# The opening of a two-layer mLSTM and attention backbone: modulation loads, the last 512 tokens' load, and the order of the first projections

## The chip, the cores and the metric

The kernel runs on one core of one Trainium2 chip. The metric is the device time of one execution in microseconds (us). The time before is the median of three runs: 2864.13 us (2863.14 to 2865.72).

The core has a matrix engine (TensorE, PE in the profile; its weight loads are PEld), a vector engine (DVE), a scalar engine (ACT), GpSimd (POOL) and SyncE (SP), which here issues the DMA transfers. Each engine works through its own instructions in order and waits on semaphores for the others.

## The reference

1024 latent tokens and 256 context tokens of width 1024 go through two layers. Each layer normalizes, modulates with vectors that a product of the conditioning with `w_ada` gives, projects with one input matrix, mixes (mLSTM heads and neighbourhood attention), projects out, and runs a squared-ReLU MLP. What the change touches is the start of layer 0:

```python
mod = silu_c @ w_ada[l] + b_ada[l]
mod_c = silu_cc @ w_ada[l] + b_ada[l]
sh1, sc1, g1, sh2, sc2, g2 = jnp.split(mod[:, None, :], N_MOD, axis=-1)
...
h = rmsnorm(x, norm1_g[l]) * (1.0 + sc1) + sh1
hc = rmsnorm(xc, norm1_g[l]) * (1.0 + sc1c) + sh1c
y, yc = token_mixers(h @ w_in[l], hc @ w_in[l], ...)
```

So before the first projection of a token there are its sum of squares, its reciprocal root, and the shift and gain of each feature, which need a pass over 8 MB of `w_ada`.

## The kernel before

**Data.** Activations lie with features on the partitions: eight feature tiles of 128, and three groups of tokens along the free axis: the 256 context tokens (group 0), latent tokens 0 to 511 (group 1) and 512 to 1023 (group 2). In the program's names, x_146 and x_147 are group 0's features 0 to 3 and 4 to 7, x_148 and x_149 those of group 1, x_150 and x_151 those of group 2. `A = range(4)` and `B = range(4, 8)` in `opening` are the lower and the upper four features.

**Products in three parts.** Every float32 factor is split into a rounded high half and a low half: `split_raw` does it for weights (`whi` on ACT, L88; `wlo` on DVE, L89), `parts` for activations (`ah` on ACT, L1112; `al` on DVE, L1113). One product is then three matrix products (L94, L95, L96), of which the last needs the low half of the activation.

**The modulation.** `ada(0, (0, 2), "mm", ap0, 6)` and `ada(0, (1, 3), ...)` are two generators, `first` and `second`: shift and gain of features 0 to 3, and of 4 to 7. Each goes through eight loads of 512 KB (`wada`, L174) in six buffers that both share. `steps(g, n)` advances one: a step multiplies a load that came six steps earlier on PE (`through`, L158, four products, eight rows in the profile) and issues the next load, as long as there is one. The fifteenth step copies the sums (L185), transposes them on PE (L188) and adds the bias and the gain (L192, L238).

**The order of the opening** is written by hand, under `manual_schedule`, and each engine follows the order of the code: the squares of groups 0 and 1 with the product that sums them (`squares`, L1657 to L1659) and their root (`rstd`, L297 and L298); the loads of group 2 and of the third chunk of the weights for keys, values and gates (`w_kvg`); the scaling by the root (`scale`, L1664); the first modulation; then `norm` (modulation L1674 or L1676, and the two halves) and `project(i, features, u)`, which adds features into the sums of token pair i (256 tokens; pair 0 is the context, 1 and 2 are group 1, 3 and 4 group 2). The lower features of pairs 0, 1 and 2 come before the second modulation is ready, and between them stand the squares of group 2 and steps of `second`. Then come the upper features of pairs 0 to 2, the scaling of group 2, and pair 3 feature by feature.

**Behind the opening** `mixers` copies the gates (L485), turns and rotates the keys (L513, L468 to L472, with the tables cos and sin; PE transposes, L525 and L336) and projects pair 4 (L94 to L96 again). From here a scheduler orders the work. In `mixers` two DMAs store the conditioning (`sscr<-silu`, L1590), in pieces of one element; a later stage reads it. Also there, `na_values` needs the two chunks of the attention's value weights (`w_nv`), the first of which the opening already loads and splits.

Of the kernel before, what the change touches and what calls it, by code (L numbers as in the profile page):

```python
# [11 lines left out]
F32 = mybir.dt.float32  # L12
# [35 lines left out]
class Kern:  # L48
# [1537 lines left out]
    def mixers(self, l, xsrc, hi, lo, need_ctx, W, accs, Wv):  # L1586
        self.wide = 0
        if l == 0:
            for v in range(2):
                self.nc.sync.dma_start(self.sscr[v, :].rearrange("(k p) -> p k", p=128), self.silu[:, :, v])  # L1590
            self.fill = self.ada(l, range(6, 10), "q")
            self.rows = self.ada_rows(l, range(4, 6), range(2))
        self.gt, self.mst, self.nst = None, {}, {}
        with self.open(name=f"mix{l}", side="right") as self.mx:
            with self.open(name=f"mkv{l}") as self.mp:
                self.cosT = self.load(self.mx, "cos", [128, 8, 32])
                self.sinT = self.load(self.mx, "sin", [128, 8, 32])
                self.sel = self.load(self.mx, "sel", [128, 16])
                kv = self.mlstm_kv(l, hi, lo, W, accs)
                with self.open(name=f"gt{l}", side="right") as tp_:  # L1600
                    gates = self.gates(l, tp_)
                    next(gates)

                    with self.tc.issue_after(self.normed.ins) if l == 0 else contextlib.nullcontext():
                        for i in range(NT // 2):
                            next(kv)
                            if i > 2:
                                next(gates)
                        next(kv)
                    values = self.na_values(l, hi, lo, Wv + self.value_weights(l, range(len(Wv), 2)))  # L1610
                    next(gates)
                    next(gates)
                    run_all(values)
                    with self.behind():
                        run_all(gates)
                W = self.joint_weights(l, 0)
                with self.behind():
                    first = self.project_j(W, 0, hi, lo, 512 if need_ctx else 256)
                with self.open(name=f"mout{l}") as self.mb:
                    self.setup_out(l)  # L1620
                    with self.behind():
                        run_all(kv)
                    Wq, keys = self.mlstm_out(l, hi, lo, need_ctx, W, first)
            with self.open(name=f"na{l}") as self.np_:
                yh, yl = self.alloc_act()
                W, xt = [], []
                self.na(l, hi, lo, need_ctx, Wq, keys, self.ahead(l, 0 if need_ctx else 1, xsrc, yh, yl, W, xt))
        return yh, yl, W, xt

    def opening(self, xp, ap0, xsrc, hi, lo):  # L1630
# [53 lines left out]
        q, A, B, accs = [[], [], []], range(4), range(4, 8), {}  # L1684

        def project(i, ks, u):
            accs[i] = self.project_g(W, i, hi, lo, "q", accs.get(i), ks, (u,))

        run_all(squares(0, q[0]))
        more = squares(1, q[1])  # L1690
# [3 lines left out]
        steps(first, 1)  # L1694
        steps(more, 1)
        steps(first, 1)
        self.load_x(x, xsrc, (2,))
        nc.sync.dma_start(raws[2][:], d["w_kvg"][0][:, 1728:])
        r1 = self.rstd(*q[1])
        scale(0, r0)  # L1700
        for z in range(2):
# [4 lines left out]
        for z in range(6):  # L1706
            steps(first, 1)
            steps(second, 1)
        self.less_last(raws[2], chunks[2][1], 288)
        steps(first, 1)  # L1710
        norm([(0, f) for f in A])
        for u in range(2):
            project(0, A, u)
        rest = squares(2, q[2])
        norm([(1, f) for f in A])
        for i in (1, 2):
            for u in range(2):
                steps(rest, 1)
                project(i, A, u)
                steps(second, 1)  # L1720
        r2 = self.rstd(*q[2])
        W.append(self.split_raw(raws[2], chunks[2][1]))
        steps(second, 4)
        scale(2, r2, range(3))
        steps(second, 1)
        norm([(0, f) for f in B])
        for u in range(2):
            project(0, B, u)
        norm([(1, f) for f in B])
        for i in (1, 2):  # L1730
            for u in range(2):
                project(i, B, u)
        scale(2, r2, range(3, KT))
        norm([(2, f) for f in range(KT)])
        accs[3] = [self.bank("mm") for _ in range(2)]
        for k in range(KT):
            for u in range(2):
                project(3, (k,), u)
        return W, accs, self.value_weights(0, range(1))

    def run(self):
        nc, d = self.nc, self.d
        PS = bass.MemoryType.PSUM
        with self.open(name="pad", side="right") as pad, self.open(name="const") as self.cp, self.open(name="w") as self.wp, \
# [12 lines left out]
            xsrc = d["xT"]  # L1757
            hi, lo = self.alloc_act()
            with self.open(name="x0") as xp, self.open(name="sp0") as self.sp, self.open(name="ada0") as ap0, self.tc.manual_schedule():
                W, accs, Wv = self.opening(xp, ap0, xsrc, hi, lo)  # L1760
            self.ntmp = 3
            for l in range(DEPTH):
                need_ctx = l < DEPTH - 1
                groups = (0, 1, 2) if need_ctx else (1, 2)
                yh, yl, W, xt = self.mixers(l, xsrc, hi, lo, need_ctx, W, accs, Wv if l == 0 else [])
                mod, A = self.mod, self.A
                hid, xmid = hids[l], xmids[l]
                ada = chain(*(self.ada_rows(*a) for a in ((l, range(10, 12), range(2)), (l + 1, range(4), range(2)), (l + 1, range(4, 12), range(1))) if need_ctx))
# [271 lines left out]
```

## Time and profile before

| what | value |
|---|---|
| median of three runs | 2864.13 us |
| the profiled execution | 2859.85 us |
| its span, first to last instruction | 2857.9 us |
| granted PE clock, mean | 0.995 |
| instructions | 45593 |
| moved by DMA | 497.39 MB, mean 174 GB/s |

The profiled execution is one run, 4.3 us below the median of the others. Rows of the timeline give the start in us from the span's start, the duration, the engine, the source line, the operation with its output and inputs, how many such instructions the row merges, and in brackets how long the engine had been idle and what ended that. SPq is SyncE's queue of DMA issues; its durations are those of issuing. Rows of stages give the busy time of PE, PEld, DVE, ACT and POOL, then the granted clock, the DMA engines' busy share and GB/s.

### The profile page before, as it was taken

Reading aid. Unit: us, or ns where it says so; the run is one execution under the profiler, and the core shown is the slowest. Engines: PE = TensorE matmul, PEld = TensorE weight load, DVE = VectorE, ACT = ScalarE, POOL = GpSimd, SP = SyncE. Lnnn points to the kernel's source line nnn. Section 1 sums busy time; section 2 is a strip of 40 time slices with the busy share of each in tenths; the row PEclk is TensorE's granted clock in tenths of the full one; section 3 lists DMA queues with packets and bytes.
Section 4 is the critical chain, followed back from the end, with each engine's and each line's share of the span. In section 5 each row is a group of like instructions: output and inputs, shape, how many; then the busy total and the mean of one; then the engine's idle time right before and its main releaser. Section 6 shows DMA issues by size and latency. Waiting matters only on the chain. (4 is left out here: it accounts for less than half of the span.)

```text
span 2857.9 us, 45593 instructions
## 1 busy us (share of the span) xinstructions
PE 2807.8 (98%) x16560; PEld 2375.8 (83%) x16560; DVE 2201.7 (77%) x4909; ACT 1276.6 (45%) x2472; POOL 111.9 (4%) x191
## 2 busy tenths in 40 slices
PE   7999999999999999999999999999999999999998
PEld 4877778888888888888889988878988788888888
DVE  5779988776698777689878778878786887768774
ACT  4333335565453333434545333335564533344453
POOL 0100000011000000000000101000010000000000
PEclk8999999999999999999999999999999999999999
DMA  7333333336447555798977222223355454479672
GB/s 243 125 132 128 133 104 108 91 114 203 138 149 246 198 195 192 247 341 295 328 264 279 71 70 88 72 76 120 113 156 193 130 183 155 145 263 320 200 256 97
DMA packets 279263, 497.39 MB, mean 174 GB/s; under 512 B 23648, under 2 KB 119904, under 8 KB 279040
## 3 DMA queue, kind: packets, MB, share of 16 engines
q1 hardware_dynamic: 279040, 494.50, 51.8%
q8 instruction: 130, 2.13, 0.3%
q14 instruction: 93, 0.76, 0.1%
HBM read 398.82 MB, written 95.59 MB: 173 GB/s over the span
## 5 line engine op out<-in xcount | busy, mean ns | idle before, releaser
L94 PE MATMUL q<-ah,whi 128*128 128x512 f32 (+1 forms) x1472 | 549.4, 373 | 0.5 <-ACT whi L1112 0.5
L96 PE MATMUL q<-ah,wlo 128*128 128x512 f32 (+1 forms) x1472 | 547.0, 372 | 0.7 <-DVE wlo L1113 0.5
L95 PE MATMUL q<-al,whi 128*128 128x512 f32 (+1 forms) x1472 | 547.6, 372 | 0.0
L94 PE MATMUL mm<-ah,whi 128*128 128x512 f32 (+1 forms) x1120 | 387.0, 346 | 0.4 <-DVE nq L859 0.2
L95 PE MATMUL mm<-al,whi 128*128 128x512 f32 (+1 forms) x1120 | 384.8, 344 | 0.0
L96 PE MATMUL mm<-ah,wlo 128*128 128x512 f32 (+1 forms) x1120 | 384.6, 343 | 0.0
L96 PEld LDWEIGHTS q<-ah,wlo 128*128 128x128 f32 x1472 | 277.3, 188 | 49.9 <-DVE wlo L1113 1.3
L94 PEld LDWEIGHTS q<-ah,whi 128*128 128x128 f32 x1472 | 277.5, 188 | 49.7 <-issue 1.7
L95 PEld LDWEIGHTS q<-al,whi 128*128 128x128 f32 x1472 | 277.5, 189 | 48.4 <-issue 1.4
L94 PE MATMUL mm<-whi,ah 128*128 128x512 f32 (+2 forms) x832 | 308.0, 370 | 1.6 <-ACT va L810 1.6
L95 PE MATMUL mm<-wlo,ah 128*128 128x512 f32 (+2 forms) x832 | 297.9, 358 | 0.4 <-DVE wlo L89 0.3
L96 PE MATMUL mm<-whi,al 128*128 128x512 f32 (+2 forms) x832 | 297.9, 358 | 0.0
L94 PEld LDWEIGHTS mm<-ah,whi 128*128 128x128 f32 x1120 | 212.0, 189 | 28.0 <-issue 2.0
L96 PEld LDWEIGHTS mm<-ah,wlo 128*128 128x128 f32 x1120 | 212.0, 189 | 25.1 <-issue 0.2
L95 PEld LDWEIGHTS mm<-al,whi 128*128 128x128 f32 x1120 | 212.0, 189 | 24.6 <-issue 0.2
L1112 ACT CAST ah<-raw 128x512 fp32r<-128x512 f32 (+1 forms) x264 | 143.5, 566 | 126.0 <-PE q L96 51.8
L1113 DVE TENSOR_TENSOR al<-raw,ah 128x512 fp32r<-128x512 f32 (+1 forms) x264 | 157.8, 622 | 29.9 <-ACT ah L1112 29.2
L94 PEld LDWEIGHTS mm<-whi,ah 128*128 128x128 f32 x832 | 157.1, 189 | 27.1 <-ACT va L810 2.4
L96 PEld LDWEIGHTS mm<-whi,al 128*128 128x128 f32 x832 | 156.9, 189 | 23.8
L95 PEld LDWEIGHTS mm<-wlo,ah 128*128 128x128 f32 x832 | 157.3, 189 | 21.3 <-DVE wlo L89 1.8
L94 PE MATMUL q<-th,whi 128*128 128x512 f32 x384 | 150.4, 392 | 2.1 <-DVE s L1277 2.0
L95 PE MATMUL q<-x,whi 128*128 128x512 f32 x384 | 150.6, 392 | 1.1 <-DVE x L1113 1.1
(306 smaller groups left out, 5237.3 us busy)
## 6 DMA issues: line engine op xcount, KB each, us to landing
raw<-w SPq DMA_DIRECT2D x168, 512.0 KB
raw<-hid SPq DMA_DIRECT2D x104, 512.0 KB
wada<-w_adaT SPq DMA_DIRECT2D x96, 512.0 KB
wraw<-w SPq DMA_DIRECT2D x80, 512.0 KB
hid<-hb SPq DMA_DIRECT2D x128, 256.0 KB
hid<-ht SPq DMA_DIRECT2D x96, 256.0 KB
w<-gscr SPq DMA_DIRECT2D x36, 512.0 KB
wada<-w_ada SPq DMA_DIRECT2D x32, 512.0 KB
```

Source lines behind the costliest of these rows:

```text
L94: mm(out, lh, rh, start=start, stop=False, skip_group_check=True)
L95: mm(out, lh, rl, start=False, stop=False, skip_group_check=True)
L96: mm(out, ll, rh, start=False, stop=stop, skip_group_check=True)
L1112: ins = self.nc.scalar.copy(hi, src)
L1113: self.nc.vector.tensor_sub(lo, src, fview(hi))
```

## The change

It reorders the opening and two places of `mixers`; no computation is added or taken out.

- The loads of group 2 move from before the modulation loop to behind the last load of `second`. The third `w_kvg` chunk's load moves into that loop, at its fourth round.
- Two steps of `second` stand right behind the first modulation, two behind the lower features of pair 0, and one behind each of pair 1's features, which are projected one by one for both halves of the pair. The final step stands between the two halves of pair 2.
- The squares of group 2 and their root stand behind the upper features of pair 0, among the modulation of group 1's upper features. Pairs 1 and 2 then take these feature by feature.
- Sums of pair 3 come from the other bank tag by `project` itself.
- The first chunk of the value weights is only loaded in the opening; it is split in `mixers`, after the second round of keys (i == 1).
- The conditioning store is issued behind the opening's last `parts` (`issue_after` places instructions behind a given one in the order, where they are on its engine).

```diff
     def mixers(...):
         if l == 0:
-            for v in range(2):
-                self.nc.sync.dma_start(self.sscr[v, :].rearrange("(k p) -> p k", p=128), self.silu[:, :, v])
+            with self.tc.issue_after(self.normed.ins):
+                for v in range(2):
+                    self.nc.sync.dma_start(self.sscr[v, :].rearrange("(k p) -> p k", p=128), self.silu[:, :, v])
...
                             if i > 2:
                                 next(gates)
+                            if Wv and i == 1:
+                                Wv = [self.split_raw(Wv[0], 1024)]
...
     def opening(...):
-            accs[i] = self.project_g(W, i, hi, lo, "q", accs.get(i), ks, (u,))
+            accs[i] = self.project_g(W, i, hi, lo, "q" if i < 3 else "mm", accs.get(i), ks, (u,))
...
-        self.load_x(x, xsrc, (2,))
-        nc.sync.dma_start(raws[2][:], d["w_kvg"][0][:, 1728:])
         r1 = self.rstd(*q[1])
...
         for z in range(6):
             steps(first, 1)
             steps(second, 1)
-        self.less_last(raws[2], chunks[2][1], 288)
+            if z == 3:
+                nc.sync.dma_start(raws[2][:], d["w_kvg"][0][:, 1728:])
         steps(first, 1)
+        steps(second, 2)
+        self.load_x(x, xsrc, (2,))
         norm([(0, f) for f in A])
         for u in range(2):
             project(0, A, u)
-        rest = squares(2, q[2])
+        steps(second, 2)
         norm([(1, f) for f in A])
-        for i in (1, 2):
+        for f in A:
             for u in range(2):
-                steps(rest, 1)
-                project(i, A, u)
-                steps(second, 1)
-        r2 = self.rstd(*q[2])
+                project(1, (f,), u)
+            steps(second, 1)
+        self.less_last(raws[2], chunks[2][1], 288)
         W.append(self.split_raw(raws[2], chunks[2][1]))
-        steps(second, 4)
-        scale(2, r2, range(3))
+        project(2, A, 0)
         steps(second, 1)
+        project(2, A, 1)
         norm([(0, f) for f in B])
         for u in range(2):
             project(0, B, u)
-        norm([(1, f) for f in B])
-        for i in (1, 2):
-            for u in range(2):
-                project(i, B, u)
+        run_all(squares(2, q[2]))
+        norm([(1, 4), (1, 5)])
+        r2 = self.rstd(*q[2])
+        scale(2, r2, range(3))
+        norm([(1, 6), (1, 7)])
+        for f in B:
+            for i in (1, 2):
+                for u in range(2):
+                    project(i, (f,), u)
         scale(2, r2, range(3, KT))
         norm([(2, f) for f in range(KT)])
-        accs[3] = [self.bank("mm") for _ in range(2)]
-        for k in range(KT):
+        for f in range(KT):
             for u in range(2):
-                project(3, (k,), u)
-        return W, accs, self.value_weights(0, range(1))
+                project(3, (f,), u)
+        raw = self.wp.tile([128, 1024], F32, name="wraw", bufs=WRAW)
+        nc.sync.dma_start(raw[:], d["w_nv"][0, :, :1024])
+        return W, accs, raw
```

On SP, the DMA queue of the opening, from the first modulation loads on, before (x_150 and x_151 are the last 512 tokens, wada 128x2x512 the opening's modulation loads, sscr the conditioning store):

```order
L174 DMA wada<-w_ada 128x2x512 x8
L1584 DMA x_150<-xT 128x4x512
L1584 DMA x_151<-xT 128x4x512
L1698 DMA wraw_174<-w_kvg 128x576
L174 DMA wada<-w_ada 128x2x512 x6
L1590 DMA sscr<-silu 128x8x1 x2
L174 DMA wada<-w_ada 128x4x256
L174 DMA wada<-w_ada 128x2x512 x2
L74 DMA wraw<-w_nv 128x1024 x2
L174 DMA wada<-w_ada 128x4x256
L132 DMA cos<-cos 128x256
```

and in the changed kernel, at the same place:

```order
L174 DMA wada<-w_ada 128x2x512 x12
L1711 DMA wraw_174<-w_kvg 128x576
L174 DMA wada<-w_ada 128x2x512 x4
L1584 DMA x_150<-xT 128x4x512
L1584 DMA x_151<-xT 128x4x512
L1747 DMA wraw<-w_nv 128x1024
L1591 DMA sscr<-silu 128x8x1 x2
L132 DMA cos<-cos 128x256
L132 DMA sin<-sin 128x256
L132 DMA sel<-sel 128x16
L174 DMA wada<-w_ada 128x4x256
L74 DMA wraw<-w_nv 128x1024
```

All sixteen modulation loads now precede the last 512 tokens; the two stores follow these and the first value weights, and precede the rotation tables and the second value weights.

On ACT, the middle of the opening before, from the last cast of group 1's lower features (ah_97) to the modulation of the context's upper features (x_147):

```order
L1112 CAST ah_97<-x_148 128x512
L1657 ACTIVATE tmp<-x_150 128x512 x4
L1657 ACTIVATE tmp<-x_151 128x512 x4
L297 ACTIVATE ssq<-mm,eps 128x512
L298 ACTIVATE ssq<-ssq 128x512
L88 CAST whi<-wraw_174 128x576
L1676 ACTIVATE x_147<-x_147,mod,A_333 128x256
```

and in the changed kernel, from the last cast of those upper features (ah_108) to the modulation of group 1's feature 6 (the second x_149):

```order
L1112 CAST ah_108<-x_147 128x256
L1660 ACTIVATE tmp<-x_150 128x512 x4
L1660 ACTIVATE tmp<-x_151 128x512 x4
L1679 ACTIVATE x_149<-x_149,mod,A_330 128x512
L1112 CAST ah_100<-x_149 128x512
L1112 CAST ah_103<-x_149 128x512
L297 ACTIVATE ssq<-mm,eps 128x512
L298 ACTIVATE ssq<-ssq 128x512
L1679 ACTIVATE x_149<-x_149,mod,A_330 128x512
```

The eight squares of group 2 and their root moved from ahead of the second modulation's use to behind it.

On DVE, the end of the opening before, from the last low half (al_134) to the keys of the first latent pair (kt of L471 and L472):

```order
L1113 TENSOR_TENSOR al_134<-x_151,ah_110 128x512
L536 MEMSET cst 128x64
L537 MEMSET cst 128x64
L89 TENSOR_TENSOR wlo<-wraw,whi 128x1024
L513 COPY kt<-q 128x128 x2
L468 TENSOR_TENSOR ropea<-q,cos 128x128 x2
L468 TENSOR_TENSOR ropeb<-q,sin 128x128 x2
L468 TENSOR_TENSOR ropea<-q,cos 128x128
L471 TENSOR_TENSOR kt<-ropea,ropeb 128x4x32
L472 TENSOR_TENSOR kt<-ropea,ropeb 128x4x32
```

and in the changed kernel:

```order
L1113 TENSOR_TENSOR al_134<-x_151,ah_110 128x512
L513 COPY kt<-q 128x128 x2
L468 TENSOR_TENSOR ropea<-q,cos 128x128 x2
L468 TENSOR_TENSOR ropeb<-q,sin 128x128 x2
L89 TENSOR_TENSOR wlo<-wraw,whi 128x1024
L471 TENSOR_TENSOR kt<-ropea,ropeb 128x4x32
L472 TENSOR_TENSOR kt<-ropea,ropeb 128x4x32
```

The low half of the value weights stands behind the rotation's products instead of ahead of them, and the two memsets went further back.

More of the change, by code (lines that the diff above doesn't have):

```diff
@@ L1759, in run @@
             with self.open(name="x0") as xp, self.open(name="sp0") as self.sp, self.open(name="ada0") as ap0, self.tc.manual_schedule():
-                W, accs, Wv = self.opening(xp, ap0, xsrc, hi, lo)
+                W, accs, raw = self.opening(xp, ap0, xsrc, hi, lo)
             self.ntmp = 3
@@ L1764, in run @@
                 groups = (0, 1, 2) if need_ctx else (1, 2)
-                yh, yl, W, xt = self.mixers(l, xsrc, hi, lo, need_ctx, W, accs, Wv if l == 0 else [])
+                yh, yl, W, xt = self.mixers(l, xsrc, hi, lo, need_ctx, W, accs, [raw] if l == 0 else [])
                 mod, A = self.mod, self.A
```

## The prediction

> **What bounds the kernel now.** First the page's busy shares, then the waits of TensorE (PE) after the opening, which is the first 80 us. The columns of the second view are engine, tile and line, what it waited for, then us in total, times and the longest.
>
> ```profile
> PE 2807.8 (98%) x16560; PEld 2375.8 (83%) x16560; DVE 2201.7 (77%) x4909; ACT 1276.6 (45%) x2472; POOL 111.9 (4%) x191
> ```
>
> ```profile
> PE q L1028 <- DVE S L1017: 5.3, 9, 1.4
> PE q L163 <- DMA wada<-w_ada: 2.1, 2, 1.2
> ```
>
> PE is busy 98% of the span, and these are its two costliest waits in 2777 us. Behind the opening, PE sets the pace and its order is unchanged, so whatever the opening ends earlier should arrive at the end nearly whole. The question is the moment at which PE begins the first piece that the change leaves alone, the key and value projection of the last 256 tokens. That is the last row of PE's timeline (columns: start, us, instruction, idle time before it):
>
> ```profile
> 23.70 1.08 PE L158 MATMUL mm<-wada,silu 128*32 128x256 f32 x8 [0.66 <-DMA wada<-w_ada]
> 25.06 1.08 PE L158 MATMUL mm<-wada,silu 128*32 128x256 f32 x8 [0.28 <-DMA wada<-w_ada]
> 26.83 0.66 PE L188 MATMUL mm<-consts,arow 128*128 128x128 f32 x2 [0.69 <-DVE arow L185]
> 29.16 0.61 PE L94 MATMUL q<-whi,ah 128*128 128x288 f32 x1 [1.67 <-ACT ah L1112]
> ...
> 34.09 0.29 PE L96 MATMUL q<-whi,al 128*128 128x288 f32 x1
> 37.48 2.05 PE L1659 MATMUL mm<-tmp,ones 128*128 128x512 f32 x2 [3.10 <-DVE tmp L1658]
> ...
> 40.05 0.44 PE L94 MATMUL q<-whi,ah 128*128 128x288 f32 x1
> 40.29 0.44 PE L95 MATMUL q<-wlo,ah 128*128 128x288 f32 x1
> ...
> 45.64 0.29 PE L95 MATMUL q<-wlo,ah 128*128 128x288 f32 x1
> 45.77 0.29 PE L96 MATMUL q<-whi,al 128*128 128x288 f32 x1
> 46.00 0.64 PE L158 MATMUL mm<-wada,silu 128*32 128x256 f32 x8
> 46.57 1.12 PE L1659 MATMUL mm<-tmp,ones 128*128 128x512 f32 x2
> ...
> 52.41 2.37 PE L158 MATMUL mm<-wada,silu 128*32 128x256 f32 x40
> 55.92 0.41 PE L188 MATMUL mm<-consts,arow 128*128 128x128 f32 x2 [1.14 <-DVE arow L185]
> 58.00 0.40 PE L94 MATMUL q<-whi,ah 128*128 128x288 f32 x1 [1.67 <-ACT ah L1112]
> ...
> 79.81 0.38 PE L94 MATMUL q<-whi,ah 128*128 128x288 f32 x1
> ```
>
> L158 multiplies a load of the modulation weights, eight rows to a load. The second half's last loads are multiplied at 52.41, and the projection of features 4 to 7 can only start at 58.00. Products follow each other by 0.24 us around 40 us (40.05, 40.29) and by 0.13 around 45.7. Why the loads are so late stands in SP's queue and in the DMA rates over 0 to 80 us (slices of 2 us):
>
> ```profile
> 19.13 1.01 SPq L1584 DMA_DIRECT2D x<-xT  x2
> ...
> 30.48 6.91 SPq L1590 DMA_DIRECT2D sscr<-silu  x2
> ```
>
> ```profile
> GB/s 19 233 385 383 387 401 402 387 387 388 386 387 389 384 385 391 393 379 386 116 2 17 40 72 215 395 410 390 176 6 0 0 0 0 0 0 162 100 0 250
> ```
>
> The last 512 tokens (2 MB) go ahead of the second half's weights, the two conditioning stores go ahead of its last two loads, and for about 10 us (38 to 48) almost no bytes move, though there is more to load.
>
> **The change part by part.** *Loads.* Loads land 1.36 us apart (23.70 to 25.06), the first half's last at 25.06. With the tokens out of the way and a store behind, the second half's eight follow directly: 25.06 + 8 x 1.36, plus 0.77 for the third weight chunk (288 of 512 KB), gives 36.7 for the last. The tokens' halves, 2.72 us each, land at 39.4 and 42.1. Six buffers are shared, and the seventh load is released by PE's multiply of the first, at about 28.4; five loads (6 us) are then still in flight, so the queue does not run dry. I price that at nothing, between 0 and 3 us (the spare time until PE wants the last load, below).
>
> *PE up to the second modulation.* Two loads are multiplied right after the transposes (27.49). A load takes 2.37 / 5 = 0.47 us at full clock, so 0.95 at half clock; the pair ends at 29.4, nearly inside the idle time up to 29.16. The first projection's 24 products took 29.16 to 34.22 (34.09 + 0.13) and now end at 34.4. PE's 3.1 us of idle before 37.48 goes, because the squares it waited for now stand later. An L158 group between projections costs 46.57 - 45.77 - 0.13 = 0.67, with a second load behind it 1.14: 35.6. Then four times six products and one load, 4 x (6 x 0.13 + 0.67) = 5.8: 41.4. Those 24 took 0.21 us each, since most ran at half clock; if PE, now without a pause ahead of them, runs them at full clock, their second half takes 1.57 instead of some 2.6, and it is 40.3. I take 41.0; either way the last load (36.7) is there.
>
> *To the projection of features 4 to 7.* Twelve products (1.57) cover the copy of the sums, then from the transpose to the first product it is 58.00 - 55.92 = 2.08, covered by twelve more. 41.0 + 1.57 + 2.08 = 44.65 instead of 58.00: **13.35 us earlier**.
>
> *What is late next.* The squares of the last 512 tokens were ready long before; now they come behind this point, on ACT, and everything that follows is a chain of ACT and DVE:
>
> ```profile
> 35.47 4.26 ACT L1657 ACTIVATE tmp<-x 128x512 f32<-128x512 f32 x8
> 50.93 0.69 ACT L297 ACTIVATE ssq<-mm,eps 128x512 f32<-128x512 f32 x1 [11.20 <-PE mm L1659]
> 51.65 0.63 ACT L298 ACTIVATE ssq<-ssq 128x512 f32<-128x512 f32 x1
> ...
> 59.56 0.41 ACT L1112 CAST ah<-x 128x256 fp32r<-128x256 f32 x1 [0.51 <-DVE x L1674]
> 59.88 0.81 ACT L1676 ACTIVATE x<-x,mod,A 128x512 f32<-128x512 f32 x1
> 60.72 0.62 ACT L1112 CAST ah<-x 128x512 fp32r<-128x512 f32 x1
> ```
>
> ```profile
> 39.76 0.69 DVE L1658 TENSOR_TENSOR tmp<-tmp 128x512 f32<-128x512 f32 x1 [0.35 <-ACT tmp L1657]
> ...
> 63.21 0.54 DVE L1674 TENSOR_SCALAR x<-x,A,mod 128x512 f32<-128x512 f32 x1
> 63.67 1.46 DVE L1113 TENSOR_TENSOR al<-x,ah 128x512 fp32r<-128x512 f32 x2
> 65.05 3.09 DVE L1664 TENSOR_TENSOR x<-x,ssq 128x512 f32<-128x512 f32 x5
> 68.06 0.54 DVE L1674 TENSOR_SCALAR x<-x,A,mod 128x512 f32<-128x512 f32 x1
> ...
> 74.03 1.47 DVE L1113 TENSOR_TENSOR al<-x,ah 128x512 fp32r<-128x512 f32 x2
> 75.76 1.51 DVE L89 TENSOR_TENSOR wlo<-wraw,whi 128x1024 fp32r<-128x1024 f32 x1
> ...
> 78.39 0.28 DVE L468 TENSOR_TENSOR ropea<-q,cos 128x128 f32<-128x128 f32 x1
> 78.58 0.28 DVE L471 TENSOR_TENSOR kt<-ropea,ropeb 128x128 f32<-128x128 f32 x1
> 78.78 0.28 DVE L472 TENSOR_TENSOR kt<-ropea,ropeb 128x128 f32<-128x128 f32 x1
> ```
>
> The context's casts end at 59.97 - 13.35 = 46.6; the eight squares take 4.26 (50.9; the tokens landed at 42.1), the last addition 0.7 (51.6), its product 1.12 (52.75). Meanwhile ACT does one modulation (0.81) and two casts (0.62 and about 0.55) until 52.9. Logarithm and exponential: 52.28 - 50.93 = 1.35, so 54.25. On DVE three scales at 0.60 (1.81), a modulation (63.67 - 63.21 = 0.46) and two subtractions (65.05 - 63.67 = 1.38) give 57.9, where the five remaining scales start. Before they started at 65.05. From there the order is the old one: 75.50 - 65.05 = 10.45 us, all DVE, to the last low half: **68.35 instead of 75.50**. So of 13.35 us, 6.2 are given back, because the squares (4.3) with their sum and root (3.3), formerly beside PE's second half, now stand in the chain. PE, which sees its products feature by feature, is ready earlier than DVE from here on.
>
> *The value split later.* From the last low half to the second rotated key was 79.06 - 75.50 = 3.56 us. The split (L89) stays inside that stretch, now behind the rotation's products; only two memsets (75.76 - 75.50 = 0.26) and one extra rope product (78.58 - 78.39 = 0.19) leave: 3.11. Its price is bounded by 0 and 1.5 (its duration, if ACT's half came late); I take 0, since ACT has only four small copies ahead of its half, and DVE six products. What queues behind the later split are the next weight loads, released at 71 instead of 77, still ahead of the old times.
>
> *The sum*: 7.15 + 0.45 = 7.6; I use **7.5 us**. The profiled execution took 2859.85 us (span 2857.9), so it would be 2852.35. The median of the runs is 2864.13, 4.3 above that execution; the same 7.5 off it gives **2856.6**, which I predict.
>
> **The clock as a term.** The columns that matter here are the granted clock and, behind it, DMA share and GB/s:
>
> ```profile
> 40.00:42.00 2.00, 2.00 (x11) 2.00 (x9) 0.46 (x1) 0.00 (x0) 0.00 (x0) 0.50 0.26 2
> ...
> 58.00:60.00 2.00, 2.00 (x9) 1.29 (x9) 1.49 (x4) 1.49 (x5) 0.00 (x0) 1.00 0.02 6
> 60.00:62.00 2.00, 2.00 (x9) 1.86 (x10) 1.57 (x3) 1.97 (x4) 0.19 (x3) 0.59 0.00 0
> 62.00:64.00 2.00, 2.00 (x11) 2.00 (x10) 1.47 (x4) 1.30 (x4) 0.00 (x0) 0.56 0.00 0
> ```
>
> After idle pieces of 1.14 and 1.67 us (rows 55.92 and 58.00), PE ran at half clock from 60.4 to 63.6. The changed order leaves PE pauses of up to 1.8 us near 49 to 52 and near 61, and 3 us before the keys, so such stretches can come there. The Trainium skill, "TensorE: Matmul & The Clock Gate", section "Why this matters for your kernels", asks only for no idle gap above about 3 us between bursts. By that the pauses inside the opening would never halve the clock. The trace here disagrees with it, since 1.67 us sufficed; by the rule the sum stays as it is, by the trace the first rival below has a chance.
>
> **The rivals.**
> - *Half clock takes part back* (15%). A stretch of 3.2 us at 0.24 instead of 0.13 us a product costs 13 products against 25: 1.5 us each. Around 50 us it is hidden by the DVE chain; one in the last DVE-bound stretch and one in the next projection cost 3 together: 2859.6. For it speaks 60 to 64 above; against it that the 3 us pause before 79.81 did not do it before.
> - *The change does not bring the second half forward enough* (8%). If the shared buffers let the queue run dry, each us beyond 41 at which the last load lands is a us lost; 4 us late gives 2860.6. Against it: from 10 to 18 us, before the tokens were issued, such loads ran at 385 to 400 GB/s.
> - *It is hidden anyway* (8%): the next stage has a wait that does not move, such as weights that now load in another order: 2863 to 2864. Against it: the few waits quoted above.
> - *Slower* (7%): the stores, now issued behind all loads, stand ahead of the rotation tables and the next value weights in SP's queue. From 43.5 they should take the 10 us that they took before, and the tables land near 55. DVE's next wait for them comes behind the first low half of the last tokens, at 62. Each us later than 62 costs one; the kernel is slower from 69.5 on, if the stores take 25 us. At 35 us it would be 2874.
>
> **How the numbers follow.** The forecast has 62%, with its own range 2854.6 to 2858.4 (a gain of 9.5 to 5.7: the clock's 1 us either way, and 1 us for ACT and DVE disturbing each other). The range takes in the first two rivals and the early end (full clock in the first projection, and all of the sum's small covers holding): 2853 to 2861.5. About 0.2% (5.7 us) is what a measurement can tell from no change. Faster: the forecast and a little of the first rival, 66%. Same: the rest of it, the second and third, 26%. Slower: 8%.
>
> **What would show it.** The second L188 near 42.6 instead of 55.92; the squares on ACT from 46.6 to 50.9; five scales at 57.9 instead of 65.05; the last low half at 68.4; the projection of the last 256 tokens at 72.3 instead of 79.81; DMA at 385 GB/s without a hole until 43, and the hole then behind the loads. It is wrong if L158 waits for its loads after 30 us, if DVE waits for the tables, or if the lead of 7.5 us at 80 is not there at the end.

## The result, and the profile after

The changed kernel takes 2853.97 us (median of six runs, 2852.49 to 2855.54). The kernel before took 2863.48 us beside it (six runs). The ratio is 0.997, with a 95% interval of 0.996 to 0.998: **9.5 us faster**, where 7.5 were forecast and 2856.6 us predicted. The time lies in the stated range (2853 to 2861.5), and the gain at the upper edge of the forecast's own 5.7 to 9.5. The profiled execution of the changed kernel took 2853.93 us, its span 2851.9. The page's busy shares show nothing of it, since PE has the same work in 6 us less:

```profile
PE 2806.3 (98%) x16560; PEld 2373.4 (83%) x16560; DVE 2201.0 (77%) x4909; ACT 1276.3 (45%) x2472; POOL 110.6 (4%) x191
```

The answer stands in the opening. PE's timeline of the changed kernel (start, us, instruction, idle time before it and what ended it):

```profile
25.21 1.08 PE L158 MATMUL mm<-wada,silu 128*32 128x256 f32 x8 [0.28 <-DMA wada<-w_ada]
26.93 0.66 PE L188 MATMUL mm<-consts,arow 128*128 128x128 f32 x2 [0.64 <-DVE arow L185]
27.52 1.94 PE L158 MATMUL mm<-wada,silu 128*32 128x256 f32 x16
...
33.65 1.07 PE L158 MATMUL mm<-wada,silu 128*32 128x256 f32 x16
...
40.32 0.64 PE L158 MATMUL mm<-wada,silu 128*32 128x256 f32 x8
...
42.58 0.38 PE L188 MATMUL mm<-consts,arow 128*128 128x128 f32 x2
...
44.63 0.40 PE L94 MATMUL q<-whi,ah 128*128 128x288 f32 x1
...
48.94 3.74 PE L1662 MATMUL mm<-tmp,ones 128*128 128x512 f32 x8
...
57.11 0.40 PE L96 MATMUL q<-whi,al 128*128 128x288 f32 x1 [0.76 <-DVE al L1113]
...
61.96 0.40 PE L96 MATMUL mm<-whi,al 128*128 128x288 f32 x1 [1.39 <-DVE gend L371]
...
71.05 0.41 PE L525 MATMUL q<-consts,kt 128*128 128x128 f32 x2 [1.65 <-DVE kt L472]
...
71.66 0.38 PE L94 MATMUL q<-whi,ah 128*128 128x288 f32 x1
```

No modulation load (L158) is waited for after 25.21. The second half's transposes (L188) come at 42.58 instead of 55.92, the upper features at 44.63 instead of 58.00, and the projection of the last 256 tokens (pair 4) starts at 71.66 instead of 79.81: a lead of 8.15 us between these two traces. ACT and DVE over the same time:

```profile
46.51 4.27 ACT L1660 ACTIVATE tmp<-x 128x512 f32<-128x512 f32 x8
...
51.52 1.14 ACT L1112 CAST ah<-x 128x512 fp32r<-128x512 f32 x2
52.72 0.69 ACT L297 ACTIVATE ssq<-mm,eps 128x512 f32<-128x512 f32 x1
```

```profile
41.02 0.43 DVE L185 COPY arow<-mm 128x256 f32<-128x256 f32 x1 [3.96 <-PE mm L158]
...
50.81 0.69 DVE L1661 TENSOR_TENSOR tmp<-tmp 128x512 f32<-128x512 f32 x1 [0.35 <-ACT tmp L1660]
...
57.75 3.09 DVE L1667 TENSOR_TENSOR x<-x,ssq 128x512 f32<-128x512 f32 x5
...
66.72 1.46 DVE L1113 TENSOR_TENSOR al<-x,ah 128x512 fp32r<-128x512 f32 x2
...
69.29 1.21 DVE L89 TENSOR_TENSOR wlo<-wraw,whi 128x1024 fp32r<-128x1024 f32 x1
...
70.63 0.28 DVE L472 TENSOR_TENSOR kt<-ropea,ropeb 128x128 f32<-128x128 f32 x1
```

The squares (L1660) now stand between the context's casts and the logarithm (L297), as forecast, and DVE waits for neither the tables nor the stores. The DMA rates in slices of 2 us show why nothing waits for a load: the gap lies behind all of the opening's loads (44 to 52), and the rotation tables have followed by 58 (forecast: near 55), ten us before DVE's first rotation.

```profile
GB/s 18 240 358 402 387 400 402 389 388 384 391 384 387 390 384 389 387 388 387 385 405 121 0 38 30 62 292 386 119 0 0 0 70 193 0 72 199 0 0 43
```

### The profile page after: what moved, and what is told of

It is laid out like the page before. It is cut to its first block, busy times and chain, and to the rows that moved or that the text cites. A ratio compares the mean times of both kernels' runs of the same rounds, so it can differ in the third digit from the quotient of the medians.

```text
span 2851.9 us, 45592 instructions
## 1 busy us (share of the span) xinstructions
PE 2806.3 (98%) x16560; PEld 2373.4 (83%) x16560; DVE 2201.0 (77%) x4909; ACT 1276.3 (45%) x2472; POOL 110.6 (4%) x191
```

## The experiments

The experiments ran in three sessions, A to C, in which the kernel before had medians of 2864.22, 2864.48 and 2863.02 us. Executions of one kernel also differ in the opening: the two traces of before are 1.5 us apart at the copy of the second modulation's sums (55.35 and 53.82). They are 0.6 us apart when PE ends its pause at 37.48 and 36.85; the other 0.9 comes while PE is at half clock behind it, with a granted clock from 40 to 42 of 0.50 in the first and 0.91 in the second. So the table gives that copy (L185), the start of pair 4, and the distance between the two, which is free of that; it is to be compared among kernels of one order of work.

| kernel | L185 | pair 4 | distance | median, us | ratio to before, 95% |
|---|---|---|---|---|---|
| before | 55.35 | 79.81 | 24.46 | 2863.48 | |
| before again (A) | 53.82 | 78.47 | 24.65 | 2865.2 (one run) | |
| changed | 41.02 | 71.66 | 30.64 | 2853.97 | 0.996 to 0.998 |
| changed again (B) | 40.79 | 71.46 | 30.67 | 2855.59 | 0.9958 to 0.9980 |
| changed again (C) | 41.42 | 72.06 | 30.64 | 2856.35 | 0.9963 to 0.9984 |
| 1 changed, store ahead (A) | 49.57 | 81.08 | 31.51 | 2864.30 | 0.9995 to 1.0013 |
| 2 before, store behind (B) | 54.71 | 78.88 | 24.17 | 2863.60 | 0.9989 to 1.0007 |
| 3 before, new loads (B) | 59.58 | 83.94 | 24.36 | 2869.83 | 1.0009 to 1.0029 |
| 4 changed, pair by pair (A) | 41.62 | 72.41 | 30.79 | 2857.50 | 0.9969 to 0.9987 |
| 5 early squares, sums on POOL (A) | 41.43 | 72.60 | 31.17 | 2857.03 | 0.9966 to 0.9985 |
| 6 early squares, sums on DVE (B) | 41.23 | 71.77 | 30.54 | 2856.47 | 0.9964 to 0.9983 |
| 7 products first (C) | 41.32 | 71.97 | 30.65 | 2856.44 | 0.9970 to 0.9988 |
| 8 both 6 and 7 (C) | 41.61 | 71.06 | 29.45 | 2856.49 | 0.9967 to 0.9985 |
| 9 changed, split early (C) | 41.55 | 73.40 | 31.85 | 2858.28 | 0.9974 to 0.9992 |

**The two controls.** The kernel before once more:

> The kernel before, unchanged, for a second trace of it: the projection of the last 256 tokens starts at 79.8 within 0.3. If the lead of the change at 72 us (8.15) is the same against this trace, the 6.0 us between the two spans shown and the 9.5 between the medians differ by what happens later in single executions; then other places than the opening of this trace differ from the first one by 2 to 4 us. Rival (the opening itself varies): the start differs by 1 us or more.

and the changed kernel twice more:

> The changed kernel as it is, beside the others on the same chip. If the lead is that of the opening, the projection of the last 256 tokens starts at 71.2 to 72.4 in any execution, and the ratio to the kernel before is 0.9960 to 0.9980 again. If the first trace was a lucky one, it starts at 73 or later, or the ratio is 0.9985 or more.

> The changed kernel once more, as the measure for the three others of this call. Theory and rival alike: the logarithm at 52.4 to 52.8, the projection of the last 256 tokens at 71.2 to 72.0, ratio 0.9960 to 0.9980.

The changed kernel repeats its distance to 0.03 us (in session C its start is 0.06 us and its logarithm, at 53.12, 0.32 us beyond the expected ranges, since that opening ran later), and its gain over the median of before was 9.5, 8.9 (B) and 6.7 us (C). The kernel before started pair 4 at 78.47, not at 79.8 within 0.3: the rival, that the opening itself varies, holds. The first trace of before was nevertheless a quick execution: the second has a span of 2863.3 us instead of 2857.9, although its pair 4 starts 1.3 us sooner. So the lead at pair 4 is 6.4 to 8.35 us, depending on which of the two traces of before and of the three of the changed kernel are compared, and 7.4 between their means.

**1. The store ahead of the second half's last two loads, in the changed kernel.**

```diff
-            with self.tc.issue_after(self.normed.ins):
-                for v in range(2):
-                    self.nc.sync.dma_start(self.sscr[v, :].rearrange("(k p) -> p k", p=128), self.silu[:, :, v])
...
         steps(first, 1)
+        for v in range(2):
+            nc.sync.dma_start(self.sscr[v, :].rearrange("(k p) -> p k", p=128), self.silu[:, :, v])
         steps(second, 2)
```

> The changed kernel with only the conditioning store put back ahead of the last two modulation loads. Chain theory (the end of the opening follows the second modulation, and this follows its last load when that is late): the store takes about 10 us of DMA time, the last two loads land at about 45 and 47 instead of 35 and 37, the copy of the sums (L185) moves from 41.0 to about 47.5, and the first product of the projection of the last 256 tokens from 71.7 to 78 to 80; time 2860 to 2862, nearly all of the gain gone. Rival (there was spare time for the store, the gain is the order of the products): that product stays at 71.7 to 72.5 and the time at 2854.

The whole gain is gone, and more than was expected: L185 comes at 49.57 instead of about 47.5, pair 4 at 81.08 instead of 78 to 80, the median is 2864.30 instead of 2860 to 2862. PE's timeline and the DMA rates of this kernel:

```profile
40.25 0.64 PE L158 MATMUL mm<-wada,silu 128*32 128x256 f32 x8 [3.04 <-DMA wada<-w_ada]
45.67 1.08 PE L158 MATMUL mm<-wada,silu 128*32 128x256 f32 x8 [3.28 <-DMA wada<-w_ada]
48.42 1.08 PE L158 MATMUL mm<-wada,silu 128*32 128x256 f32 x8
```

```profile
GB/s 15 234 383 382 389 393 410 390 382 391 383 388 390 382 390 390 220 6 20 36 24 99 363 398 407 398 378 391 243 15 0 0 0 0 0 0 0 127 135 0
```

Almost nothing moves from 34 to 44, and the last load, which the changed kernel multiplies at 40.32, is multiplied at 48.42, 8.1 us later. Behind the two waits PE's granted clock is 0.50 from 42 to 50, which the expectation had no term for; what share of the excess this is was not tried apart. In the new order the store's place decides.

**2. The opposite move in the kernel before: only the store goes behind the loads.**

```diff
-            for v in range(2):
-                self.nc.sync.dma_start(self.sscr[v, :].rearrange("(k p) -> p k", p=128), self.silu[:, :, v])
...
         steps(second, 4)
+        for v in range(2):
+            nc.sync.dma_start(self.sscr[v, :].rearrange("(k p) -> p k", p=128), self.silu[:, :, v])
         scale(2, r2, range(3))
```

> The kernel before, with one edit: the conditioning store is issued behind the second half's last two loads instead of ahead of them. Nothing else is moved. Chain theory: in the old order PE reaches these loads at about 52.4 and the store's gap in the loads (38 to 48) ends before that, so it was not what PE waited for; the projection of the last 256 tokens stays at 78.2 to 79.8, and the ratio is 0.9990 to 1.0010. Rival (the store's gap ahead of the loads was the whole cost in the old order): that projection at 72 to 74, ratio 0.9970 to 0.9980.

Pair 4 at 78.88 and a ratio around 1: in the old order PE reaches these loads so late that the gap costs nothing. The rival falls.

**3. The new order of loads under the old order of the work.**

```diff
-            for v in range(2):
-                self.nc.sync.dma_start(self.sscr[v, :].rearrange("(k p) -> p k", p=128), self.silu[:, :, v])
+            with self.tc.issue_after(self.normed.ins):
+                for v in range(2):
+                    self.nc.sync.dma_start(self.sscr[v, :].rearrange("(k p) -> p k", p=128), self.silu[:, :, v])
...
-        self.load_x(x, xsrc, (2,))
-        nc.sync.dma_start(raws[2][:], d["w_kvg"][0][:, 1728:])
...
         for z in range(6):
             steps(first, 1)
             steps(second, 1)
+            if z == 3:
+                nc.sync.dma_start(raws[2][:], d["w_kvg"][0][:, 1728:])
         self.less_last(raws[2], chunks[2][1], 288)
         steps(first, 1)
+        steps(second, 2)
+        self.load_x(x, xsrc, (2,))
         norm([(0, f) for f in A])
...
-        steps(second, 4)
+        steps(second, 2)
```

> The kernel before with the changed kernel's order of loads (second half of the modulation, third weight chunk, last 512 tokens, store behind all) but with the old order of the work: the last tokens' squares stay between the projections, so PE meets them early. Chain theory (order of the loads and order of the work only pay together): the squares now wait for tokens that land at 40.5 to 42, PE stands from about 34 to 41 and runs at half clock behind that; the projection of the last 256 tokens starts at 78 to 82, ratio 0.9990 to 1.0015. Rival (the order of the loads alone is the gain): that projection at 72 to 74, ratio 0.9970 to 0.9980.

It is slower than before, by 5.4 us. PE's timeline shows the reason, a wait of 8.11 us for the squares of tokens that now land last (in the kernel before PE waited 3.10 us for them):

```profile
34.18 0.29 PE L96 MATMUL q<-whi,al 128*128 128x288 f32 x1
42.58 2.04 PE L1660 MATMUL mm<-tmp,ones 128*128 128x512 f32 x2 [8.11 <-DVE tmp L1659]
```

The direction was expected, the size was not: pair 4 came 2 us behind the expected range, and the ratio (1.0019) is above it. So the order of loads alone does not pay; it needs the new order of work. The reverse, the new order of work with the old order of loads, was not tried.

**4. Pairs 1 and 2 pair by pair instead of feature by feature, in the changed kernel.**

```diff
-        for f in B:
-            for i in (1, 2):
-                for u in range(2):
-                    project(i, (f,), u)
+        for i in (1, 2):
+            for u in range(2):
+                project(i, B, u)
```

> The changed kernel with the upper features of pairs 1 and 2 projected pair by pair, as before, not feature by feature. Chain theory (DVE sets the end of the opening): PE waits some 4 us for the low half of feature 7 at about 57.7, may then run at half clock for 3.4 us, ends pair 3 at 68.8 to 70.4 instead of 68.6, and the projection of the last 256 tokens starts at 71.7 to 72.1; time within 0.5 us of the changed kernel. Rival (feature by feature is what keeps PE going): the start is 2 us or more later than 71.66.

The rival (2 us or more later) falls: the distance grows by 0.15 us, so this part of the change is worth next to nothing here, although pair by pair PE has a stretch at half clock (below). That pair 4 starts at 72.41, beyond the 71.7 to 72.1 expected, is for the most part that opening's 0.6 us; the time could not be set against the changed kernel, which did not run in session A.

**5 to 8: what the logarithm waits for.** By the forecast, ACT's eight squares stand in the chain for 4.3 us. Experiment 5 does four of them ahead, as soon as the last tokens' first half has landed (40.5), adds them on POOL, and sums them on PE ahead of the context's upper features:

```diff
         W.append(self.split_raw(raws[2], chunks[2][1]))
+        ready = [self.sp.tile([128, 512], F32, name="tmp", bufs=self.ntmp) for _ in range(4)]
+        for f, t in enumerate(ready):
+            nc.scalar.activation(t[:], xf(x, 2, f), AF.Square)
+        for z in range(2):
+            nc.gpsimd.tensor_add(ready[2 * z][:], ready[2 * z][:], ready[2 * z + 1][:])
...
+        p2 = self.bank("mm")
+        q[2].extend((p2, 512))
+        for z in range(2):
+            nc.tensor.matmul(p2[:], self.ones[:], ready[2 * z][:], start=z == 0, stop=False)
...
```

> The changed kernel with the squares of the first four features of the last 512 tokens ahead of the second modulation (ACT waits there from 36.2 to 43.5), their sums in pairs on POOL, and their two products ahead of the upper features of the context. Chain theory (the squares stand in the chain and took 4.3 us of the lead): the logarithm on ACT starts at 50.6 to 51.0 instead of 52.72, the five scales at 55.7 to 56.0 instead of 57.75, the projection of the last 256 tokens at 69.6 to 70.0 instead of 71.66, and the kernel is 2 us faster than the changed one. Rival (DVE or PE bound that stretch anyway): the scales stay at 57.75 within 0.4.

It gained nothing: the five scales start at 58.69, where 55.7 to 56.0 were expected, and pair 4 at 72.60 instead of 69.6 to 70.0. The reason lies ahead of the chain that was meant to be shortened. The timelines of POOL and DVE in this kernel:

```profile
41.74 2.54 POOL L1730 TENSOR_TENSOR tmp<-tmp 128x512 f32<-128x512 f32 x2 [9.01 <-ACT tmp L1728]
44.22 1.17 POOL L330 MEMSET gr<- 128x1280 f32 x1
45.32 1.15 POOL L349 MEMSET gb<- 64x1280 f32 x1
46.43 1.16 POOL L350 MEMSET gm<- 64x1280 f32 x1
```

```profile
43.68 0.70 DVE L238 SCALAR_TENSOR_TENSOR A<-mod,consts 128x4 f32<-128x4 f32 x2
44.41 3.33 DVE L1677 TENSOR_SCALAR x<-x,A,mod 128x256 f32<-128x256 f32 x1
```

The sums push three memsets to 44.22 to 47.59 (in the changed kernel the last is over at 43.31), and DVE's modulation of the context (0.41 us in the other kernels) stands until they are over. So experiment 6 does the sums on DVE instead, behind the context's subtractions, with the products where they were:

> The changed kernel, with the four squares of the first four features of the last 512 tokens on ACT as soon as the third weight chunk is split (about 40.5 to 42.7), their two pair sums on DVE behind the context's subtractions (47.1 to 48.4), and all four products behind the context's upper features. Nothing is added on POOL. Chain theory (the squares cost what of them stands between the context's casts and the logarithm): four squares fewer there are 2.1 us, so the logarithm starts at 50.6 to 51.3 instead of 52.72, the five scales at 55.6 to 56.4 instead of 57.75, the projection of the last 256 tokens at 69.5 to 70.3 instead of 71.66, and the time is 1.4 to 2.1 us below the changed kernel of the same call. DVE's modulation of the context, which stood for 3.33 us while POOL's memsets ran when the sums were on POOL, takes 0.41 us again, with the memsets at 41 to 44. Rival 1 (PE or another wait is next): the five scales come earlier, the projection of the last 256 tokens does not (71.4 to 71.9). Rival 2 (DVE's two more sums take the gain back): five scales at 57.4 or later, no gain.

The modulation is back at 0.41 us, and still there is no gain: the five scales start at 57.84 and pair 4 at 71.77. The scales come as late as Rival 2 has it, but not for its reason, since DVE's last sum ends at 49.70. ACT's timeline says why:

```profile
52.80 0.69 ACT L297 ACTIVATE ssq<-mm,eps 128x512 f32<-128x512 f32 x1 [2.00 <-PE mm L1745]
```

ACT is ready 2 us earlier and now waits for PE. In the changed kernel PE finishes the context's upper features at 48.94 and then has four products of the squares, 3.74 us, which end at 52.68; the last sum on DVE ends at 51.50, which with its product would be 52.6. ACT itself is busy with two casts, queued behind its squares, until 52.66 (51.52 + 1.14). **Two chains end at the same moment**, the one through ACT's squares and PE's, and removing one shows the other. Experiment 7 takes away PE's alone, by moving the products between the context's two upper projections (the edit below); experiment 8 does both:

```diff
-        for u in range(2):
-            project(0, B, u)
+        project(0, B, 0)
         run_all(squares(2, q[2]))
+        project(0, B, 1)
```

> The changed kernel with that second edit alone: the products of the squares between the context's two upper projections; the squares stay where they are on ACT. Two-limits theory: ACT's squares end at 50.7 and the last sum at 51.5 as before, so the logarithm starts at 52.4 to 52.8, the projection of the last 256 tokens at 71.3 to 71.9, no gain. Rival (PE alone was the limit and ACT's squares cost nothing): the logarithm at 51.3 or earlier and that projection at 70.3 or earlier.

> The kernel with the early squares and the sums on DVE, and in addition the four products of the squares on PE between the context's two upper projections instead of behind both. Two-limits theory (in the changed kernel the logarithm waits for ACT's squares, 51.5 for the last sum, and at the same time for PE, which is busy with the context's projection to 48.9 and then needs 3.7 us for four products; either alone gives nothing): the sums stand at 47.9 to 49.7, the products run from 47.9 to 50.8, the logarithm starts at 50.8 to 51.3 instead of 52.7, the five scales at 55.8 to 56.3, the projection of the last 256 tokens at 69.7 to 70.3 instead of 71.5 to 71.7, and the time is 1.3 to 1.9 us below the changed kernel of the same call. Rival (DVE or PE's moved projection is next): the logarithm comes earlier, that projection does not (71.3 or later).

PE in experiment 7, then PE and ACT in experiment 8:

```profile
48.82 4.16 PE L1662 MATMUL mm<-tmp,ones 128*128 128x512 f32 x8 [1.01 <-DVE tmp L1661]
```

```profile
48.39 1.95 PE L1738 MATMUL mm<-tmp,ones 128*128 128x512 f32 x4 [0.30 <-DVE tmp L1737]
50.19 1.88 PE L1744 MATMUL mm<-tmp,ones 128*128 128x512 f32 x4
```

```profile
52.10 0.69 ACT L297 ACTIVATE ssq<-mm,eps 128x512 f32<-128x512 f32 x1 [0.94 <-PE mm L1744]
```

Either edit alone leaves the distance within 0.1 us (30.54 and 30.65 against 30.64); both together take 1.2 us off it (29.45). The two-limits theory holds. The logarithm came later than the 50.8 to 51.3 expected: at 52.10, or 51.5 with the 0.6 us taken off by which this opening ran later. PE's four products, 3.7 us without a break from 48.39, still end last. Pair 4 starts at 71.06, or 70.5 with the same 0.6 us taken off, where 69.7 to 70.3 was expected. A gain of 1.3 to 1.9 us was expected in the time of the whole kernel, and there none can be seen: 2856.49 us against 2856.35 of the changed kernel in the same session, with intervals that overlap almost wholly.

**9. The value split back in the opening.**

```diff
-                            if Wv and i == 1:
-                                Wv = [self.split_raw(Wv[0], 1024)]
...
-        raw = self.wp.tile([128, 1024], F32, name="wraw", bufs=WRAW)
-        nc.sync.dma_start(raw[:], d["w_nv"][0, :, :1024])
-        return W, accs, raw
+        return W, accs, self.value_weights(0, range(1))
```

> The changed kernel with the split of the first value weights back in the opening, as in the kernel before, instead of behind the second pair's keys. My forecast gave the later split 0.45 us: the projection of the last 256 tokens then starts at 71.9 to 72.1 instead of 71.5 to 71.7 (with the opening's own scatter, best read as its distance from the end of the last low half: 3.9 to 4.1 us instead of 3.5). Rival (the split costs nothing either way): the same distance within 0.15 us. In both cases the time is within 0.7 us of the changed kernel's.

From the end of the last low half (67.25 + 1.47 = 68.72) to pair 4 (73.40) it takes 4.68 us, and 3.48 in the changed kernel (68.18 to 71.66). That is **1.2 us** instead of 0.45, beyond the 3.9 to 4.1 expected, and the rival falls. The median is 1.9 us above the changed kernel's in the same session, where 0.7 at most was expected; the two intervals overlap. DVE and PE in experiment 9, and the granted clock (after the five busy times):

```profile
68.97 1.32 DVE L89 TENSOR_TENSOR wlo<-wraw,whi 128x1024 fp32r<-128x1024 f32 x1
...
71.81 0.28 DVE L472 TENSOR_TENSOR kt<-ropea,ropeb 128x128 f32<-128x128 f32 x1
```

```profile
70.85 0.44 PE L525 MATMUL q<-consts,kt 128*128 128x128 f32 x2 [1.26 <-ACT va L515]
72.23 0.66 PE L525 MATMUL q<-consts,kt 128*128 128x128 f32 x2 [0.95 <-DVE kt L472]
72.69 1.06 PE L336 MATMUL q<-consts,gr 128*128 128x128 f32 x4
```

```profile
72.00:74.00 2.00, 1.77 (x8) 1.80 (x9) 2.00 (x11) 1.02 (x6) 0.00 (x0) 0.52 0.46 180
```

The second rotated key is ready 72.09 - 68.72 = 3.37 us after the low half, against 70.91 - 68.18 = 2.73: 0.64 us is on DVE, 0.11 of it the split's own time (1.32 us instead of 1.21). The other 0.56 is PE at half clock from there to pair 4. Not every execution with the early split pays that: in the first trace of before the same two pauses stand, and the granted clock is 1.00 from 76 to 84:

```profile
77.83 0.44 PE L525 MATMUL q<-consts,kt 128*128 128x128 f32 x2 [1.11 <-ACT va L515]
79.21 0.41 PE L525 MATMUL q<-consts,kt 128*128 128x128 f32 x2 [0.94 <-DVE kt L472]
```

With the early split the stretch from the last low half to pair 4 is 4.02 (experiment 2), 4.20 (3), 4.31 and 4.50 (the two traces of before) and 4.68 us; with the later one it is 3.47 or 3.48 in the three traces of the changed kernel. So the later split is worth 0.5 to 1.2 us.

## Why the prediction was right

The forecast's mechanism and its steps hold; two of its numbers came out partly by luck, and they are named below.

- **The loads.** Forecast: the last one at 36.7, no dry queue. PE waits for none of them, and the rates stay near 385 GB/s until 42.
- **The second modulation and the upper features.** Forecast 42.6 and 44.65; measured 42.58 and 44.63. The second half's products end at 40.96 (40.32 + 0.64), between the bounds of 40.3 and 41.4. That this is so near the 41.0 taken is partly luck: the first projection and its two loads were over by 34.65 instead of 35.6, with PE's clock whole from about 31 on, and the four groups of six products and a load took 6.24 us (34.65 to 40.89) instead of 5.8. In this kernel PE has no pause near 37 and its granted clock is 1.00 from 32 to 90, where the first trace of before has about 7 us at half clock between 36 and 44.
- **What is late next.** Squares forecast at 46.6 to 50.9, measured 46.51 to 50.78; five scales 57.9 against 57.75; last low half 68.35 against 68.18. Of a lead of 13.37 us at the upper features, 7.32 are left at the last low half (75.50 - 68.18), so 6.05 are given back, where I said 6.2. What the forecast did not see is that PE's four products end within 0.1 us of the chain it named. So the right time came with some luck, and experiment 6 shows that a reader who shortened that chain alone would have gained nothing.
- **The split later.** The term of the sum that was mis-sized: 0.45 us forecast. The distance from the last low half to pair 4 fell from 4.31 to 3.48, by 0.83, and 0.30 of that is the split's own time, 1.21 us instead of 1.51. In the kernel before it overlaps an operation of POOL:

```profile
75.58 0.61 POOL L82 TENSOR_TENSOR wmore<-wmore 128x252 f32<-128x252 f32 x1 [14.91 <-DVE al L1113]
```

With the early split, the longer POOL's operation still runs when the split starts, the longer the split takes: 1.32 us for 0.25 us of overlap (experiment 9), 1.40 for 0.32 (3), 1.43 for 0.36 and 1.51 for 0.43 (the two traces of before). In experiment 2, where both start at 75.12, the split takes 1.23 and POOL's operation 1.69. In the changed kernel POOL's operation is over at 68.65, ahead of the split. The forecast had no term for this. With it the lead at pair 4 is 8.15 us instead of 7.5 between the first two traces.
- **The clock.** The rival "half clock takes part back" did not come: in the changed kernel the pauses at 57.11 (0.76) and 61.96 (1.39) leave the clock whole, as does the one of 1.65 at 71.05. The forecast's "3 us pause before 79.81", which spoke against this rival, was misread: PE's pauses there are 1.11 and 0.94 us (the rows at experiment 9).

```profile
60.00:62.00 2.00, 0.61 (x6) 0.38 (x4) 1.95 (x7) 0.67 (x2) 0.00 (x0) 1.00 0.00 0
62.00:64.00 2.00, 2.00 (x13) 1.79 (x14) 1.91 (x4) 2.00 (x4) 0.00 (x0) 1.00 0.00 0
```

But half clock does occur in this opening. In experiment 4 pauses of 1.57 and 1.11 us end 1.6 us apart, in experiment 9 those of 1.26 and 0.95 us 1.4 apart, and both then run at half clock. PE's pauses and the clock of experiment 4:

```profile
56.08 0.40 PE L94 MATMUL q<-whi,ah 128*128 128x288 f32 x1 [1.57 <-ACT ah L1112]
57.71 0.40 PE L96 MATMUL q<-whi,al 128*128 128x288 f32 x1 [1.11 <-DVE al L1113]
```

```profile
60.00:62.00 2.00, 2.00 (x10) 2.00 (x10) 2.00 (x5) 0.07 (x1) 0.00 (x0) 0.50 0.00 0
```

No rule comes out of these runs. The clock also fell behind pauses of 1.03 and 0.94 us that end 1.4 us apart (the second trace of before), but not behind 1.11 and 0.94 us, as close together, in the first. Single pauses of up to 1.65 us did not cost it; one of 2.24 us (experiment 2, at 37.81) did. The Trainium skill, "TensorE: Matmul & The Clock Gate", section "Why this matters for your kernels", asks for no gap above about 3 us; the changed kernel agrees with it, experiments 2, 4 and 9 do not. What decides was not tried apart.

**The store ahead of the tables.** The tables were there by 58, and the rival that ended slower had no place to act.

**The end.** The lead at pair 4 is there at the end, within the scatter. Between the first two traces it is 2857.9 - 2851.9 = 6.0 us, against the second trace of before 2863.3 - 2851.9 = 11.4, between medians 9.5, 8.9 and 6.7. So the gain is the opening's lead (6.4 to 8.35 us at pair 4, 7.4 between the means), within the scatter of the sessions. These runs can't tell 8.15 from the forecast's 7.5, and the 9.5 measured first is the largest of the three gains.

That the gain hangs on order, and that neither the loads nor the store pay alone, is shown: the loads alone lose 5.4 us (experiment 3), the store alone gives nothing (2), and the changed kernel with the store in front gives nothing either (1).

## What to carry to other kernels

When a late load is brought forward, the work that used to fill the time before it goes into the chain behind it; price that work first: here 6 of 13 us went back. The store in small pieces cost nothing in the old order, where nobody waited for what was queued behind it, and the whole gain in the new one, so the place of such a transfer has to be looked at again after each reordering. Before shortening a chain, look at every other engine's end at the same moment: here two chains ended within 0.1 us, and shortening either alone gained nothing.

## What the runs showed of the hardware that was not expected

- A DVE operation can stand still through several of POOL's. In experiment 5 a modulation of 0.41 us took 3.33 and ended at 47.74, 0.15 us after the last of three memsets that follow each other without a break. The Trainium skill, "SBUF — State Buffer", section "🔬 SBUF: two separate sides", says that DVE and GpSimd share a port pair as a lock that the one who comes first holds for its whole instruction; the trace agrees, and adds that DVE did not get in between the three. The split of the value weights, 1.21 us alone and up to 1.51 us beside POOL's operation, is a second place of this kind.
- Executions of one kernel drift apart behind the opening too. When the products of the two traces of before are matched one by one, the second is 1.5 us ahead at 72 us, 2.7 behind at 403, 4.3 at 761, 4.2 at 1406 and 5.3 at the end. Experiment 7 and the changed kernel differ only in the opening and start pair 4 within 0.3 us of each other, but the span of experiment 7 is 5.7 us longer: it is 0.8 us behind at 403 us, 2.2 at 498, 4.1 at 654, 4.4 at 761 and still 4.4 at 1406. Of the 3.6 us between 403 and 761, 2.6 are longer waits of PE for DVE's states (L1017). These waits from 480 to 770 us, first in the changed kernel, then in experiment 7 (us in total, times, longest):

```profile
PE q L1028 <- DVE S L1017: 4.3, 6, 1.3
```

```profile
PE q L1028 <- DVE S L1017: 6.9, 12, 1.5
```

A gain like the 1.2 us of experiment 8 is small beside such differences of 5 us between two spans. What starts them was not tried.
